# Grouping output stores on a saturated DMA queue: two stores of eight heads at every sixteenth head, in place of one at every eighth

## The chip, the cores and the metric

One core of a Trainium2 chip. The time is the device time of one execution in microseconds (us); the median of several executions is quoted. A profile is one execution recorded by the hardware profiler; its span leaves out some 1.8 us of the execution's time. The core's engines go by their short names: PE multiplies and transposes, DVE, ACT and POOL are the vector, scalar and GpSimd engines, SP the sync engine. HBM is the chip's main memory.

## The reference

```
attn_weights: float32 [8, 12, 1024, 1024]     v: float32 [8, 12, 1024, 64]
out = einsum('bhqs,bhsd->bhqd', attn_weights, v)      # float32 [8, 12, 1024, 64]
```

There are 96 heads. Each is a 1024 x 1024 matrix times a 1024 x 64 matrix. The weights are 403 MB, V and the output 25 MB each, so nearly all of the traffic is weights.

## The kernel before

The kernel takes four heads at a time (`q`, 24 steps) and loads their weights in two halves (`n`, 48 units), cast to bfloat16 on the way into two buffers `abf`. PE transposes each half, DVE and ACT copy the transposes out, PE multiplies and transposes back, and ACT copies the results into `osb`, a ring of ten slots of four heads each. POOL issues all transfers in the loop on one queue: weights, V for eight heads, and the output stores of eight heads (two slots).

```python
    HELD_FROM = NV - 8          # 16; NV = 24 steps of four heads
    BY_SYNC = NV - 4
    RING = 5                    # five pairs of slots
    ...
        def store(q, fours, eng, done):
            eng.wait_ge(s_out, 2 * (q + fours) + 1)
            at_slot = osb[:, ds(slot(q), fours)].rearrange("p n r d -> p n (r d)")
            eng.dma_start(
                out=out_2[q // 2] if fours == 2 else out_q[q],
                in_=at_slot if fours == 2 else at_slot[:, 0],
                **({"single_packet": True} if eng is pool else {}),
            ).then_inc(done, 16)

        def store_2(q):
            store(q, 2, pool, s_osb[q // 2 % 2] if q < HELD_FROM else s_held)
    ...
        for n in range(NU - 2):                       # POOL
            q, i = n // 2, n % 2
            if i == 0 and q % 2 == 1 and q + 1 < NV:
                for s in s_sp:
                    pool.wait_ge(s, 2 * q + 2)
                load_v((q + 1) // 2)
            pool.wait_ge(s_t[True], (n + 1) * PER_DVE)   # unit n is transposed, its buffer is free
            load_attn(n + 2)
            if i == 0 and q % 2 == 0 and 0 < q <= HELD_FROM:
                store_2(q - 2)
        for q in range(HELD_FROM, BY_SYNC, 2):
            store_2(q)
    ...
        nc.sync.sem_inc(s_free, RING)                 # SP
        for n in range(-2, NU - 2):
            ...
            nc.sync.sem_inc(s_half)
            if n >= 0 and n % 2 == 0:
                q = n // 2
                ...
                if q % 2 == 1 and 1 < q <= HELD_FROM:
                    nc.sync.wait_ge(s_osb[(q - 3) // 2 % 2], 16 * ((q - 3) // 4 + 1))
                    nc.sync.sem_inc(s_free)
        store(NV - 4, 2, nc.sync, s_end)
        store(NV - 2, 1, nc.sync, s_end)
        ...                                           # three last stores of the last four heads
        for k in range(2):
            nc.sync.wait_ge(s_osb[k], 16 * (HELD_FROM // 4))
        nc.sync.wait_ge(s_held, 16 * (BY_SYNC - HELD_FROM) // 2)
        nc.sync.wait_ge(s_end, 16 * 5)
```

SP waits for completions and passes them on: `s_half` tells PE that a load is complete, `s_free` tells ACT that a pair of slots may be written again. Because SP waits on constants, its loop is unrolled.

Of the kernel before, what the change touches and what calls it, by code (L numbers as in the profile page):

```python
# [10 lines left out]
def kernel(  # L11
# [18 lines left out]
    nc = tc.nc  # L30
# [15 lines left out]
    VB = S // VP // SB  # L46
    NV = NH // VH
    NU = 2 * NV


    HELD_FROM = NV - 8
# [4 lines left out]

    HALVED = NU - 2

    def slot(q):
        return q % NO  # L60
# [20 lines left out]
    with tc.tile_critical(no_gpsimd_drain=True):  # L81
# [18 lines left out]
        s_abf = [sem(f"s_abf{i}") for i in range(2)]  # L100
        s_second = {n: sem(f"s_second{n}") for n in range(HALVED, NU)}
        s_v0, s_v = sem("s_v0"), sem("s_v")
        s_osb = [sem(f"s_osb{i}") for i in range(2)]
# [15 lines left out]
        s_half, s_free = sem("s_half"), sem("s_free")  # L119
# [33 lines left out]
        def transpose_back(parts=((0, 4, px[0]), (4, 4, px[1]))):  # L153
            for j0, jn, ps in parts:
                for j in range(jn):
                    last = pe.matmul(  # L156
                        out=ps[:, ds(j * P, P)],
                        lhsT=ot[:, j0 + j],
                        rhs=ident,
                        is_transpose=True,  # L160
                        start=(j == 0),
                        stop=(j == jn - 1),
                    )
                last.then_inc(s_back)
# [16 lines left out]
        def wait_both(s, n):  # L181
            for x in s:
                pe.wait_ge(x, n)

        def pe_unit(i, n, loaded, it):

            pe.wait_ge(*loaded)
            for g in range(G):
                if g == GH:
                    pe.wait_ge(s_half, n)  # L190
                transpose_g(abf[i], g, n)
            wait_both(s_ot, n)
            if i == 0:
                pe.wait_ge(s_vr, it)
                odd = pe.snap((it - 1) % 2)
                with pe.If(odd > 0):
                    spread_v(1, po + px)
                with pe.Else():
                    spread_v(0, po + px)
                wait_both(s_vbf, it * 2)  # L200
            transpose_back()
            wait_both(s_last, n)
            for hp in range(2):
                for h in range(2):
                    for half in range(2):
                        outs = po[hp][ds(half * D, D), ds(h * GH * VP, GH * VP)]
                        last = multiply(outs, 2 * hp + h, half)
                last.then_inc(s_m[hp])

        pe.wait_ge(s_const, 1 + VH)  # L210
        with nc.Fori(1, NV + 1, 1, engines=(PE,)) as it:
# [4 lines left out]
            pe_unit(1, second, (s_abf[1], loaded), it)  # L216
        wait_both(s_ot, NU + 1)
        transpose_back()


        def engine(dve):
# [11 lines left out]
            def back_copy(rows, j0, jn, ps, count):  # L233

                eng.wait_ge(s_back, count)
                return copy(  # L236
                    out=rows.rearrange("p (half j) d -> p j half d", half=2)[:, ds(j0, jn)],
                    in_=ps[:, ds(0, jn * P)].rearrange("p (j half d) -> p j half d", half=2, d=D),
                )
# [59 lines left out]
            rows = osb[:, slot(NV - 1), ds(G, G)]  # L299
            back_copy(rows, 4 * k, 4, px[k], 2 * NU + k + 1).then_inc(s_fin[k])  # L300

# [13 lines left out]
        def load_attn(n):  # L315
            pieces = [(0, G)] if n < HALVED else [(0, GH), (GH, GH)]
            for g0, gn in pieces:
                pool.dma_start(  # L318
                    out=abf[n % 2][:, ds(g0, gn)].rearrange("p g s -> p (g s)"),
                    in_=attn_q[n // 2][:, ds((n % 2 * G + g0) * S, gn * S)],  # L320
                ).then_inc(s_abf[n % 2] if g0 == 0 else s_second[n], 16)

        def load_v(iv):
            pool.dma_start(  # L324
                out=vr.rearrange("p two b x -> p two (b x)"), in_=v_2[iv]
            ).then_inc(s_v, 16)
# [12 lines that stand above are left out]
# [14 lines left out]
        for h in range(VH):  # L353
# [9 lines left out]
            ).then_inc(s_const)  # L363
        for n in range(NU - 2):
# [4 lines that stand above are left out]
                load_v((q + 1) // 2)  # L369
            pool.wait_ge(s_t[True], (n + 1) * PER_DVE)  # L370
            load_attn(n + 2)
            if i == 0 and q % 2 == 0 and 0 < q <= HELD_FROM:
                store_2(q - 2)
        for q in range(HELD_FROM, BY_SYNC, 2):
            store_2(q)
# [11 lines left out]
        nc.sync.sem_inc(s_free, RING)  # L387
        for n in range(-2, NU - 2):

            if n + 2 < HALVED:  # L390
                nc.sync.wait_ge(s_abf[n % 2], 16 * ((n + 2) // 2 + 1))
            else:
                nc.sync.wait_ge(s_second[n + 2], 16)
# [3 lines that stand above are left out]
                if q % 2 == 1 and q + 1 < NV:  # L397
                    nc.sync.wait_ge(s_v, 16 * ((q + 1) // 2))
                    nc.sync.sem_inc(s_vr, 2)
                if q % 2 == 1 and 1 < q <= HELD_FROM:  # L400
                    nc.sync.wait_ge(s_osb[(q - 3) // 2 % 2], 16 * ((q - 3) // 4 + 1))
                    nc.sync.sem_inc(s_free)
        store(NV - 4, 2, nc.sync, s_end)
        store(NV - 2, 1, nc.sync, s_end)
        rows = osb[:, slot(NV - 1)].rearrange("p (u half j) d -> p u half j d", u=2, half=2)
# [41 lines left out]
```

## Time and profile before

| | before |
|---|---|
| time, median of 3 | 1054.85 us (1054.56 to 1054.90) |
| span of the profiled execution | 1053.1 us |
| busiest compute engine | PE, 70% |
| share of the 16 DMA engines held by POOL's queue | 99.1% |
| HBM read / written | 427.82 / 25.17 MB |

The chain of waits is the view to read here. Each of its rows gives a start, a duration and what was waited for, so a row "DMA abf" ends (start plus duration) when a load of weights has landed. In mid-stream, every landing in the chain is that of the second half of a step of four heads, so between two lie two loads, with a V load, a store or nothing more. I call the distance between two landings an interval, and the time from the first landing in mid-stream (near 86.7 us) to the last load of weights the stream. Before, the first is 59.47 + 27.21 = 86.68, in a line that the prediction shows, and the last is

```profile
1001.80 29.87 DMA abf<-in_attn_weights_dram
```

at 1031.67, so the stream takes 944.97 us from the unrounded records. What follows it is the tail, in which the last 8.39 MB of output leave, and then the end, from the last completion to the last instruction.

### The profile page before, as it was taken

How to read it: one execution, taken by the hardware profiler on the slowest of the kernel's cores; microseconds unless marked ns; L12 is line 12 of the kernel's file. 1: busy time of each engine (PE TensorE's matmuls, PEld its weight loads, DVE VectorE, ACT ScalarE, POOL GpSimd, SP SyncE). 2: the span in 40 equal slices, each digit the busy share in tenths (PEclk: the TensorE clock that was granted, in tenths of full speed). 3: DMA queues.
4: the chain of work that ended last, by engine and by line, in shares of the span. 5: the costliest groups of instructions: out<-in, count | busy, mean ns of one | idle time of the engine just before them, and what ended most of it. 6: DMA issues, size and time to landing. Idle time of an engine off the chain costs nothing.

```text
span 1053.1 us, 16530 instructions
## 1 busy us (share of the span) xinstructions
PE 738.0 (70%) x6920; PEld 692.4 (66%) x6920; DVE 388.8 (37%) x582; ACT 410.3 (39%) x493; POOL 45.1 (4%) x80
## 2 busy tenths in 40 slices
PE   0787677676697568667768757765776866875885
PEld 0686676565686567656668657765766866865874
DVE  0453343333353234333334324433333433532542
ACT  0354344433353334333335334433333533533542
POOL 1000000000000000000000000000000000000000
PEclk9989888898798888889879888888887987988998
DMA  9999999999999999999999999999999999999998
GB/s 235 224 217 218 218 244 219 219 214 249 231 214 251 215 219 258 217 219 230 243 217 210 259 217 218 259 219 219 248 217 217 218 211 225 219 208 230 206 216 339
DMA packets 14330, 240.19 MB, mean 228 GB/s; under 512 B 1269, under 2 KB 1781, under 8 KB 4725
## 3 DMA queue, kind: packets, MB, share of 16 engines
q0 software_dynamic: 12912, 233.84, 99.1%
q1 hardware_dynamic: 1413, 6.29, 1.5%
q8 instruction: 2, 0.03, 0.0%
q14 instruction: 3, 0.02, 0.0%
HBM read 427.82 MB, written 25.17 MB: 430 GB/s over the span
## 4 chain that ended last, share of the span: by engine, by line
DMA 75%; PE 22%; issue 1%; DVE 0%; SPq 0%; ACT 0%; POOL 0%; DVEq 0%
DMA abf<-in_attn_weights_dram 72%; PE bank L129 21%; DMA osb<-in_v_dram 3%; PE bank L171 1%; PE bank L156 0%; DVE vbf L229 0%; SPq L384 0%; PE bank L144 0%; DVE at L250 0%; DVE osb L236 0%; ACT ot L262 0%; POOL abf L318 0%; DVEq L249 0%; DVE vr L308 0%; DVEq L283 0%
## 5 line engine op out<-in xcount | busy, mean ns | idle before, releaser
L129 PE MATMUL bank<-ident,abf 128*128 128x128 f32 x3072 | 454.1, 318 | 273.6 <-DMA abf<-in_attn_weights_dram 264.4
L129 PEld LDWEIGHTS bank<-ident,abf 128*128 128x128 f32 x3072 | 444.2, 214 | 286.8 <-DMA abf<-in_attn_weights_dram 276.2
L250 DVE COPY at<-bank 128x1024 bf16<-128x1024 bf16 x480 | 320.4, 689 | 463.8 <-PE bank L129 460.0
L250 ACT COPY at<-bank 128x1024 bf16<-128x1024 bf16 x288 | 288.8, 1012 | 419.9 <-PE bank L129 419.9
L171 PE MATMUL bank<-at,vbf 128*64 128x256 bf16 x3072 | 215.0, 278 | 0.0
L171 PEld LDWEIGHTS bank<-at,vbf 128*64 128x64 bf16 x3072 | 196.8, 108 | 13.4 <-DVE at L250 4.0
L262 ACT COPY ot<-bank 128x512 f32<-128x512 f32 x48 | 28.1, 586 | 174.2 <-PE bank L171 174.2
L262 DVE COPY ot<-bank 128x512 f32<-128x512 f32 x48 | 33.2, 692 | 151.3 <-PE bank L171 151.3
L156 PE MATMUL bank<-ident,ot 128*128 128x128 f32 x392 | 52.2, 276 | 32.9 <-DVE vbf L229 32.1
L156 PEld LDWEIGHTS bank<-ident,ot 128*128 128x128 f32 x392 | 43.4, 141 | 45.0 <-DVE vbf L229 43.9
L236 ACT COPY osb<-bank 128x512 f32 (+1 forms) x97 | 52.2, 589 | 27.1 <-PE bank L156 26.3
L318 POOL DMA_DIRECT2D abf<-in_attn_weights_dram x50 | 27.3, 546 | 692.4 <-PE bank L129 691.4
L229 DVE CAST vbf<-bank 128x512 bf16<-128x512 f32 x48 | 30.9, 686 | 6.5 <-PE bank L144 6.5
L229 ACT CAST vbf<-bank 128x512 bf16<-128x512 f32 x48 | 25.8, 589 | 11.8 <-PE bank L144 11.8
L144 PE MATMUL bank<-vr,spread 32*128 32x512 bf16 x384 | 25.8, 377 | 0.0
L324 POOL DMA_DIRECT2D vr<-in_v_dram x11 | 7.8, 706 | 234.9 <-PE bank L144 234.9
L250 ACT ACT_TABLE_LOAD x12 | 15.4, 1283 | 1.3 <-SPq L81 1.1
L144 PEld LDWEIGHTS bank<-vr,spread 32*128 32x128 bf16 x384 | 10.2, 92 | 6.7
L308 DVE CAST vr<-osb 128x4096 bf16<-128x4096 f32 x1 | 2.3, 2294 | 30.4 <-DMA osb<-in_v_dram 30.4
L331 POOL DMA_DIRECT2D out_dram<-osb x10 | 7.2, 717 | 30.4 <-ACT osb L236 30.4
L355 POOL TENSOR_SCALAR_AFFINE_SELECT spread<-spread 32x512 bf16<-32x512 bf16 x4 | 2.5, 631 | 0.6
L236 DVE COPY osb<-bank 128x512 f32<-128x512 f32 x1 | 0.7, 692 | 3.1 <-PE bank L156 3.1
(8 smaller groups left out, 2.1 us busy)
## 6 DMA issues: line engine op xcount, KB each, us to landing
abf<-in_attn_weights_dram POOLq DMA_DIRECT2D x46, 4096.0 KB, 33.3
out_dram<-osb POOLq DMA_DIRECT2D x10, 2048.0 KB, 29.5
vr<-in_v_dram POOLq DMA_DIRECT2D x11, 1024.0 KB, 17.2
abf<-in_attn_weights_dram POOLq DMA_DIRECT2D x4, 2048.0 KB, 24.4
out_dram<-osb SPq DMA_DIRECT2D x1, 2048.0 KB, 13.7
osb<-in_v_dram SPq DMA_DIRECT2D x1, 1024.0 KB
out_dram<-osb SPq DMA_DIRECT2D x1, 1024.0 KB, 15.8
osb<-in_v_dram SPq DMA_DIRECT2D x1, 768.0 KB
```

The lines of the kernel that those rows point to most:

```text
L129: last = pe.matmul(out=pt[g % 4][:, k], lhsT=words[:, k], rhs=ident, is_transpose=True, start=(k == 0), stop=(k == KW - 1),)
L144: last = pe.matmul(out=ps, lhsT=spread[rows, b], rhs=vr[rows, two, b], start=(b == 0), stop=(b == VB - 1),)
L156: last = pe.matmul(out=ps[:, ds(j * P, P)], lhsT=ot[:, j0 + j], rhs=ident, is_transpose=True, start=(j == 0), stop=(j == jn - 1),)
L171: last = pe.matmul(out=outs, lhsT=vbf[:, 2 * kw + par, h], rhs=at[:, ds(half * GH, GH), kw, ds(h * VP, VP), par], start=(n == 0), stop=(n ...
L229: copy(out=vbf[:, :, h], in_=ps.rearrange("p (k d) -> p k d", k=SB)).then_inc(s_vbf[e])
L236: return copy(out=rows.rearrange("p (half j) d -> p j half d", half=2)[:, ds(j0, jn)], in_=ps[:, ds(0, jn * P)].rearrange("p (j half d) -> ...
L250: ins = copy(out=at[:, g].rearrange("c k j two -> c (k j two)"), in_=bank[g % 4].bitcast(bf16),)
L262: copy(out=ot.rearrange("c j (h p) -> c h j p", h=VH)[:, ds(2 * e, 2)], in_=po[e].rearrange("c (h j p) -> c h j p", h=2, j=GH),).then_inc( ...
L318: pool.dma_start(out=abf[n % 2][:, ds(g0, gn)].rearrange("p g s -> p (g s)"), in_=attn_q[n // 2][:, ds((n % 2 * G + g0) * S, gn * S)],).th ...
L324: pool.dma_start(out=vr.rearrange("p two b x -> p two (b x)"), in_=v_2[iv]).then_inc(s_v, 16)
L331: eng.dma_start(out=out_2[q // 2] if fours == 2 else out_q[q], in_=at_slot if fours == 2 else at_slot[:, 0], **({"single_packet": True} if ...
L355: pool.affine_select(out=spread[ds(h * VP, VP)], in_=spread[ds(h * VP, VP)], compare_op=mybir.AluOpType.not_equal, fill=1.0, base=0, patte ...
```

## The change

The intent is to turn the DMA engines from loading to storing four times in the loop instead of eight. The bytes stay. SP's bookkeeping has to follow: it now waits for two stores and frees two pairs of slots at once.

```diff
-            if i == 0 and q % 2 == 0 and 0 < q <= HELD_FROM:
+            if i == 0 and q % 4 == 0 and 0 < q <= HELD_FROM:
+                store_2(q - 4)
                 store_2(q - 2)
...
-                if q % 2 == 1 and 1 < q <= HELD_FROM:
-                    nc.sync.wait_ge(s_osb[(q - 3) // 2 % 2], 16 * ((q - 3) // 4 + 1))
-                    nc.sync.sem_inc(s_free)
+                if q % 4 == 1 and 1 < q <= HELD_FROM + 1:
+                    for k in range(2):
+                        nc.sync.wait_ge(s_osb[k], 16 * (q // 4))
+                    nc.sync.sem_inc(s_free, 2)
```

## The prediction

> **What bounds the kernel now.** I first read the page's engine shares and DMA rows, then the chain of waits, then the timeline of POOL, which issues nearly every transfer.
>
> ```profile
> span 1053.1 us, 16530 instructions
> PE 738.0 (70%) x6920; PEld 692.4 (66%) x6920; DVE 388.8 (37%) x582; ACT 410.3 (39%) x493; POOL 45.1 (4%) x80
> ...
> q0 software_dynamic: 12912, 233.84, 99.1%
> ...
> HBM read 427.82 MB, written 25.17 MB: 430 GB/s over the span
> ```
>
> No compute engine is over 70%, while the queue that POOL feeds holds all 16 DMA engines for 99.1% of the span. 452.99 MB pass through HBM at 430 GB/s. The kernel is a stream of transfers, and work on the other engines is free unless it makes the stream pause.
>
> The chain of waits in order of time (start us, us, what) says how steady the stream is. Each "DMA abf" row ends when a load of weights has landed, so sums of start and duration are a clock: 59.47 + 27.21 = 86.68, 95.05 + 35.14 = 130.19, and so on.
>
> ```profile
> 59.47 27.21 DMA abf<-in_attn_weights_dram
> ...
> 95.05 35.14 DMA abf<-in_attn_weights_dram
> ...
> 139.97 34.49 DMA abf<-in_attn_weights_dram
> 174.47 0.04 issue
> 174.51 10.02 PE bank L129 x64
> 184.53 0.29 issue
> 184.81 33.19 DMA abf<-in_attn_weights_dram
> ...
> 226.37 35.61 DMA abf<-in_attn_weights_dram
> ...
> 795.50 33.03 DMA abf<-in_attn_weights_dram
> ...
> 836.89 30.29 DMA abf<-in_attn_weights_dram
> ```
>
> Between two such landings lie two loads of 8.39 MB (float32 in HBM) and either a V load of 2.10 MB, an output store of 2.10 MB, or, late in the kernel, nothing. The row of PE between them is not a cost: while PE transposes, the next load is already moving.
>
> The POOL timeline (start us, us, engine, line, operation, what) gives the queue's order:
>
> ```profile
> 95.05 0.53 POOL L318 DMA_DIRECT2D abf<-in_attn_weights_dram  x1 [14.19 <-PE bank L129]
> 120.61 0.53 POOL L318 DMA_DIRECT2D abf<-in_attn_weights_dram  x1 [25.02 <-PE bank L129]
> 124.94 0.71 POOL L331 DMA_DIRECT2D out_dram<-osb  x1 [3.80 <-ACT osb L236]
> 139.97 0.56 POOL L318 DMA_DIRECT2D abf<-in_attn_weights_dram  x1 [14.32 <-PE bank L129]
> 162.12 0.71 POOL L324 DMA_DIRECT2D vr<-in_v_dram  x1 [21.59 <-PE bank L144]
> ```
>
> The load issued at 139.97 lands at 174.46; the load issued at 120.61 and the store of 124.94 are ahead of it in the queue. So the interval 130.19 to 174.47 holds load, store, load; the next one, to 218.00, holds V, load, load.
>
> **What the Trainium skill says.** "DMA: Bandwidth & Descriptors", section "Where 436 GB/s comes from", puts the ceiling of a core's 16 DMA engines at 435 GB/s. The trace agrees: the interval without V or store, 828.53 to 867.18, is 38.65 us for 16.78 MB, 434 GB/s. So loads have nothing left to give. The same page, "Anatomy of one DMA", fits a fixed cost of about 2 us to each DMA, mostly waiting for the write's receipt. In this trace that is not visible on the stream, since other transfers are queued behind: a V interval costs only 4.9 us over the plain one (below), 0.07 us over its bytes. The section "Two DMAs through the same engine are not ordered" says that an engine's read and write sides are separate queues and pipelined, which fits such joins being nearly free. I found no page that gives a cost for turning from reading HBM to writing it; that cost is what the change could save, and only the trace can size it.
>
> **The change part by part.** *Bytes and instructions.* Ten POOL stores of 2048 KB before, ten after; no descriptor, load or compute instruction differs, as the instruction orders of the two kernels also show: only the places of the stores in POOL's order differ. Eight of the ten are in the loop (the two held ones are issued after the last load either way). After it, they come as four pairs: the queue reads load, store, store, load at every sixteenth head, where it read load, store, load at every eighth.
>
> *What a store costs the stream now.* The eight store intervals, from the chain, are 44.28, 43.97, 43.64, 43.59, 43.55, 43.72, 43.82 and 43.56 us: sum 350.13, mean 43.77. V intervals are 43.50 to 43.58, about 43.53. Plain ones are 38.64 and 38.62. So a V load costs 43.53 - 38.63 = 4.90 us and a store 43.77 - 38.63 = 5.14 us. At 434 GB/s, 2.10 MB need 4.83 us. A store thus has an excess of 0.31 us over its bytes and 0.24 over an equal load; eight stores 2.5 us over bytes, 1.9 us over loads. The completion records of single DMA engines in the trace show where it sits: the last of the 16 engines gets 0.1 to 0.4 us later in the load just ahead of most stores (the spread between first and last engine's completions grows from 1.14 us at 130.19 to 2.15 us at 785.01, stepwise at stores and never at V loads). That looks like a cost of the turn from reading to writing.
>
> *What halving the turns saves.* If the whole excess belongs to the turn and each pair pays it once, four of eight turns go: 4 x 0.24 to 4 x 0.31 = 0.95 to 1.25 us. If the excess belongs to the bytes written, nothing goes. The steps are uneven (0.75 us in the first store interval, 0.02 in the fifth), so they may depend on chance alignment. I take two thirds: about 0.8 us saved.
>
> *Waits.* POOL waited 8 times for ACT's copy before a store, 3.80 us each, 30.4 us in total in the waits. Of a pair, the first store's data are eight heads old and need no wait; the second has the old wait. Only four waits of 3.8 us stay: 15.2 us less POOL waiting, worth nothing on the path, since the next load's issue comes 15 us after the store anyway (139.97 against 124.94).
>
> *The handshake.* SP now frees two slots at once, after the pair, at every fourth step of four heads. ACT needs the first freed slot at the step of heads 40 to 43; it is freed two loads after the pair issued at the step of heads 16, about nine loads of over 19.3 us ahead. All later ones are similarly early (eight loads at least). ACT's waits on osb name only PE now (26.3 us, never a store) and should still.
>
> Sum: 1054.85 - 0.8 = about 1054.05 us.
>
> **The rivals.**
>
> *A. Turns are expensive and the pair hides one: a gain of several us.* Against: the whole excess of all eight stores is 2.5 us, so even removing all of it could not give 2%, which is 21 us. With half the turns, at most 1.25 us: 1053.6.
>
> *B. The longer block of writes starves the loads.* A pair is about 10 us in which no weights arrive. For: PE would idle that much longer before one unit. Against: PE already waits for loads 264 us in total; the weights' buffer can be refilled as soon as PE has transposed it (8 to 10.5 us), and the next load is then issued with half of the 19.3 us of the current one still to go, so the queue does not run dry. A pair makes that margin larger for the load behind it. In return, the intervals without a store have only loads: four loads at 19.3 us each; PE's work per unit is 738.0 / 48 = 15.4 us. The late stretch 785 to 867 runs like that now without a gap. Time: unchanged. A dry queue at each pair would have to add 5 us x 4 = 20 us even to reach 2%, and I see no mechanism.
>
> *C. Back-to-back writes are slower than single ones (a buffer toward HBM fills).* The end of the kernel has 8.39 MB of stores with nothing between: from the last weights at 1031.66 to the last completion at 1051.47 is 19.81 us, 423 GB/s, or 4.95 us per 2.10 MB, on par with 5.14 for a lone store. So at most +0.1 us per second store: 1055.2.
>
> *D. SP gets stuck on the pair's completion and releases the second half of a load late.* SP waits for the stores only after a load has landed that was queued two loads later, on the same queue; the stores are done by some 24 us by then. Time: unchanged.
>
> **Range and chances.** The mechanism bounds the saving at some 1.3 us (2.5 if all stray excess vanished), the losses at a few tenths, and three timed runs of before spread over 0.34 us. I expect 1054.05 us, with 1053.0 to 1055.2 holding it 8 times in 10. A move of 2% is 21 us, eight times the whole excess of all stores; for faster or slower by that much I leave 1% each, for something I have not seen, and 98% for within 2%.
>
> **What would show each step right or wrong.** In the chain of waits of after, intervals between landings should be about 43.5 (V), 38.6 (plain) and four of about 48.5 to 48.8 (pair: 38.63 + 2 x 4.83 + one turn of 0.3 = 48.6). A pair interval of 48.9 or more (38.63 + 2 x 5.14) would say that the excess goes with the bytes, and the saving is nil. The DMA share should stay at 99%, the totals of HBM traffic equal, POOL's wait for ACT fall to about 15 us, ACT's osb wait keep naming PE. The prediction is wrong if ACT waits for a store, if PE waits for SP in mid-kernel, if a DMA slice of the page falls below 9 in the middle, or if a plain interval becomes longer than 38.7 us.

## The result, and the profile after

| | before | after |
|---|---|---|
| time, median of 6 | 1054.80 us (1053.95 to 1055.22) | 1054.74 us (1054.38 to 1057.07) |
| span of the profiled execution | 1053.1 us | 1053.1 us |

The ratio of after to before is 1.0003, with a 95% interval of 0.999 to 1.0016. It is the ratio of the mean times, 1055.06 and 1054.71 us, so not quite that of the medians; one run of 1057.07 us pulls it above 1. The change made no difference that the clock shows.

The page of after, its totals first:

```profile
span 1053.1 us, 16527 instructions
...
q0 software_dynamic: 12912, 233.84, 99.0%
...
q14 instruction: 3, 0.02, 0.0%
HBM read 427.82 MB, written 25.17 MB: 430 GB/s over the span
```

Bytes and packets are those of before. There are three instructions fewer, which at first sight means nothing. (I come back to them and to the "instruction" queue.)

The chain of waits of after, with its columns start us, us, what:

```profile
57.50 28.99 DMA abf<-in_attn_weights_dram
...
176.97 35.25 DMA abf<-in_attn_weights_dram
...
220.58 40.20 DMA abf<-in_attn_weights_dram
...
271.27 33.05 DMA abf<-in_attn_weights_dram
...
312.68 30.29 DMA abf<-in_attn_weights_dram
...
352.80 33.72 DMA abf<-in_attn_weights_dram
...
394.88 40.29 DMA abf<-in_attn_weights_dram
...
1002.27 28.42 DMA abf<-in_attn_weights_dram
```

The landings are at 212.22, 260.78, 304.32, 342.97, 386.52 and 435.17. So a pair interval takes 48.56 us (260.78 - 212.22), a V interval 43.54, a plain one 38.65, and the next pair interval 48.65. The stream runs from 86.49 to 1030.69 and takes 944.20 us, 0.77 us less than before. That is the predicted saving, and the stream began 0.20 us earlier as well, yet the span is the same to 0.1 us. The time gained is spent after the stream.

POOL's timeline around the first pair and its wait in the list of waits (engine, line, waited for: us in total, times, longest):

```profile
203.21 0.53 POOL L319 DMA_DIRECT2D abf<-in_attn_weights_dram  x1 [25.72 <-PE bank L130]
203.73 0.71 POOL L332 DMA_DIRECT2D out_dram<-osb  x1
207.54 0.72 POOL L332 DMA_DIRECT2D out_dram<-osb  x1 [3.10 <-ACT osb L237]
220.58 0.55 POOL L319 DMA_DIRECT2D abf<-in_attn_weights_dram  x1 [12.32 <-PE bank L130]
```
```profile
POOL out_dram L332 <- ACT osb L237: 12.4, 4, 3.1
```
```profile
ACT osb L237 <- PE bank L157: 26.2, 25, 1.1
```

The first store of the pair goes out at once, the second waits 3.1 us for ACT, and the next load is issued 13 us later, with the queue full. ACT's only wait before writing `osb` is still for PE, never for a store.

Where the stream's gain went can be read from the records of completions and of SP's instructions in the trace (this is my own listing of them, not a profile view):

```
                               before     after
last weights landed           1031.66   1030.69
last store completed          1051.47   1051.00     tail 19.81 -> 20.31 us
last instruction              1053.11   1053.06     end   1.64 ->  2.06 us

SP instruction 79, counted from 0 in the profile:
before   issue of the last store      previous one ended 1045.04, this began 1045.46
after    branch after the last wait   previous one ended 1051.04, this began 1051.46
```

Half a microsecond went in the tail and 0.42 us at the end. The 0.42 us is a pause of SP ahead of its 80th instruction. The pause is there before, too, but before it delays the issue of a store that would have queued anyway (in b_hand, below, that store is issued 0.27 us earlier, and the tail is 19.80 us). In after SP has 90 instructions instead of 93, and the same pause falls behind the last completion, where everything waits for it.

### The profile page after: what moved, and what is told of

It reads as the page before. It is cut to its first block, busy times and chain, and to the rows that moved or that the text cites. A ratio compares the mean times of both kernels' runs of the same rounds, so it can differ in the third digit from the quotient of the medians. Undisturbed runs are those within 1.5% of the kernel's fastest.

```text
span 1053.1 us, 16527 instructions
## 1 busy us (share of the span) xinstructions
PE 725.6 (69%) x6920; PEld 679.8 (65%) x6920; DVE 387.9 (37%) x582; ACT 410.1 (39%) x493; POOL 45.0 (4%) x80
## 4 chain that ended last, share of the span: by engine, by line
DMA 76%; PE 22%; issue 1%; DVE 0%; SPq 0%; ACT 0%; POOL 0%; DVEq 0%
DMA abf<-in_attn_weights_dram 73%; PE bank L130 20%; DMA osb<-in_v_dram 3%; PE bank L172 1%; PE bank L157 0%; DVE vbf L230 0%; SPq L386 0%; PE bank L145 0%; DVE at L251 0%; DVE osb L237 0%; ACT ot L263 0%; POOL abf L319 0%; DVEq L250 0%; DVE vr L309 0%; DVEq L284 0%
## 5 line engine op out<-in xcount | busy, mean ns | idle before, releaser
L130 PE MATMUL bank<-ident,abf 128*128 128x128 f32 x3072 | 441.8, 313 | 284.8 <-DMA abf<-in_attn_weights_dram 279.5
L130 PEld LDWEIGHTS bank<-ident,abf 128*128 128x128 f32 x3072 | 431.9, 214 | 298.0 <-DMA abf<-in_attn_weights_dram 291.3
L332 POOL DMA_DIRECT2D out_dram<-osb x10 | 7.2, 719 | 12.4 <-ACT osb L237 12.4
```

Source lines behind the costliest of these rows:

```text
L130: last = pe.matmul(out=pt[g % 4][:, k], lhsT=words[:, k], rhs=ident, is_transpose=True, start=(k == 0), stop=(k == KW - 1),)
L332: eng.dma_start(out=out_2[q // 2] if fours == 2 else out_q[q], in_=at_slot if fours == 2 else at_slot[:, 0], **({"single_packet": True} if ...
```

## The experiments

The clock cannot resolve any of this: executions of one kernel differ by up to 2.7 us. The profiles can, since their intervals repeat within hundredths except where stores are. So each experiment is read from its profile, and its time is given beside it. The experiments ran in three groups on three chips, each beside a run of the kernel before; every group has profiles with lone stores and with pairs. Theories: the turn theory of the prediction (each turn from loading to storing has a price, which a pair pays once); the theory that the excess goes with the bytes stored or is chance; the place theory for the end (the pause belongs to a place in SP's instruction stream); and, later, that issuing a store early is what helps.

### a_again: the changed kernel once more

No edit.

> The changed kernel once more, to see whether the stream gain of its first profile repeats. Turn theory (each turn from loading to storing costs 0.24 to 0.31 us beyond the bytes, a pair pays it once): the four intervals with a pair again 48.5 to 48.75 us, time 0.7 to 1.0 us below before. No-effect theory (the excess goes with the bytes, or the steps of the first profile of before were chance): pair intervals 48.9 or more, or before's own intervals shorter this time; time within 0.3 us of before.

Measured: 1055.05 us (5 runs) against 1055.16 (9 runs), ratio 1.0. Pair intervals 48.44, 48.50, 48.63, 48.62; stream 943.79 us. The stream's gain repeats, and the time again does not show it.

### b_again: the kernel before against itself

No edit.

> The kernel before against itself: how far two sets of runs of one kernel lie apart, and whether its eight store intervals repeat. Turn theory: store intervals again average about 43.75 us, time within 0.2 us of before. Chance theory: the uneven steps (0.75 us in the first interval, 0.02 in the fifth) move or vanish, and the average store interval differs from 43.77 by more than 0.1.

Measured: 1054.61 us (1054.25 to 1056.39) against 1055.16, which is how far two sets of runs of one kernel lie apart. This was more than I expected. The mean store interval is 43.76 us, as in the first profile (43.77), and the stream 944.90. But the intervals with a large excess are others: the first has 0.02 us this time, the third 0.54. So the total repeats and its steps do not.

### apart: the same pairs, with a load between the two stores

```diff
-            if i == 0 and q % 4 == 0 and 0 < q <= HELD_FROM:
-                store_2(q - 4)
-                store_2(q - 2)
+            if q % 4 == 0 and 0 < q <= HELD_FROM:
+                store_2(q - 4 + 2 * i)
```

> The same two stores at every sixteenth head, but with one load of weights between them, so eight turns again while everything else of the change (late first store, two slots freed at once) stays. Turn theory: the gain goes, time equals before, 0.7 to 1.0 us above the changed kernel. If lateness or the handshake mattered: equal to the changed kernel. No-effect theory: all three equal within 0.3 us.

Measured: 1055.84 us against 1055.16, ratio 1.0004; stream 945.50 us, 1.3 to 1.7 above the two profiles of after, end 2.06 us. The chain of waits around the first two stores:

```profile
178.68 33.72 DMA abf<-in_attn_weights_dram
...
220.75 35.67 DMA abf<-in_attn_weights_dram
...
267.04 37.79 DMA abf<-in_attn_weights_dram
```

The landings are at 212.40, 256.42 and 304.83. Taking away only the adjacency takes away the stream's gain, so neither the lateness of the stores nor the handshake made it. The four intervals with the first store average 44.12 us, those with the second and V 48.40: the first store of each group costs 5.47 us over a plain interval and the second 4.86 over a V interval. A price per turn would have charged both the same.

### quad: four stores back to back

```diff
-            if i == 0 and q % 4 == 0 and 0 < q <= HELD_FROM:
-                store_2(q - 4)
-                store_2(q - 2)
+            if i == 0 and q % 8 == 0 and 0 < q <= HELD_FROM:
+                for k in (8, 6, 4, 2):
+                    store_2(q - k)
...
-                if q % 4 == 1 and 1 < q <= HELD_FROM + 1:
+                if q % 8 == 1 and 1 < q <= HELD_FROM + 1:
                     for k in range(2):
-                        nc.sync.wait_ge(s_osb[k], 16 * (q // 4))
-                    nc.sync.sem_inc(s_free, 2)
+                        nc.sync.wait_ge(s_osb[k], 32 * (q // 8))
+                    nc.sync.sem_inc(s_free, 4)
```

> Four stores back to back at every thirty-second head: two turns in place of eight. Turn theory: 6 x 0.24 to 0.31 = 1.4 to 1.9 us below before; the two intervals with four stores 38.63 + 4 x 4.83 + 0.3 = 58.3 us. Bytes theory: 38.63 + 4 x 5.14 = 59.2 us and time as before. If ACT ever waits for a slot (it has one unit to spare), a wait on a DMA shows on ACT and the time rises.

Measured: 1055.35 us against 1055.16, ratio 1.0002. The two intervals are 58.80 and 58.25 us, the stream 944.00. So four in a row gain over lone stores (0.9 us) but nothing over pairs in the stream, and the expected 1.4 to 1.9 did not come. The end is 2.14 us. SP has 88 instructions here, and number 79 is a DRAIN two instructions further on, with a pause of 0.44 us ahead of it. That made the place theory likely.

### a_pad: the changed kernel with three idle SP instructions

```diff
+        s_pad = sem("s_pad")
...
+                if q in (3, 7, 11):
+                    nc.sync.sem_inc(s_pad)
                 if q % 4 == 1 and 1 < q <= HELD_FROM + 1:
```

> The changed kernel with three idle semaphore increments added to SP, so that SP again executes 93 instructions instead of 90. In the traces so far SP's instruction number 79 (counted from 0) always starts 0.4 us late: in before it is the issue of the last store, hidden behind queued stores; in the changed kernel the branch after the last completion. Place theory: the pause moves back to the last store, the distance from the last store's completion to the end of the span falls from 2.06 to about 1.64 us, and the time is 0.4 us below the changed kernel, 0.8 to 1.2 below before where the stream gain holds. Rival (the late branch comes from the new handshake or from when completions come): the distance stays at 2.06.

Measured: 1054.57 us against 1054.71, ratio 1.0. The end is 1.64 us, with SP's instruction 79 being the issue of the last store again. The place theory holds in this direction. The stream is 943.63 us, the shortest with correct stores, but the tail is 20.65 us, so the last completion still comes at 1051.12 and the expected gain of 0.8 to 1.2 us against before is not there. To the last instruction, this profile takes 965.92 us from the landing near 86.7, the least of the correct kernels (quad takes 965.95); its difference in time from before lies inside the noise, and it was not timed beside the changed kernel.

### b_hand: the new handshake alone

```diff
-                if q % 2 == 1 and 1 < q <= HELD_FROM:
-                    nc.sync.wait_ge(s_osb[(q - 3) // 2 % 2], 16 * ((q - 3) // 4 + 1))
-                    nc.sync.sem_inc(s_free)
+                if q % 4 == 1 and 1 < q <= HELD_FROM + 1:
+                    for k in range(2):
+                        nc.sync.wait_ge(s_osb[k], 16 * (q // 4))
+                    nc.sync.sem_inc(s_free, 2)
```

> The kernel before with SP's new handshake alone (two slots freed at once), stores in the old places: 90 SP instructions. Place theory: end distance 2.06 us as in the changed kernel, stream between first and last weights 944.9 us as before, time 0.4 us above before. Rival (the pairs on the queue cause the late end): end distance 1.64 us, time as before.

Measured: 1055.11 us (1055.03 to 1055.73) against 1054.71; the interval of the ratio, 0.9991 to 1.0018, still spans 1. End 2.06 us and stream 944.93, both as expected; tail 19.80. So half of the change, by itself, costs 0.42 us at the end of the profile. With a_pad, which undoes it by three idle instructions, this leaves the number of SP's instructions as the cause.

### single: sixteen stores of four heads

```diff
-            if i == 0 and q % 2 == 0 and 0 < q <= HELD_FROM:
-                store_2(q - 2)
+            if i == 0 and 0 < q <= HELD_FROM:
+                store(q - 1, 1, pool, s_osb[(q - 1) // 2 % 2])
...
-                    nc.sync.wait_ge(s_osb[(q - 3) // 2 % 2], 16 * ((q - 3) // 4 + 1))
+                    nc.sync.wait_ge(s_osb[(q - 3) // 2 % 2], 32 * ((q - 3) // 4 + 1))
...
-            nc.sync.wait_ge(s_osb[k], 16 * (HELD_FROM // 4))
+            nc.sync.wait_ge(s_osb[k], 32 * (HELD_FROM // 4))
```

> The kernel before with a store of four heads at every fourth head: sixteen bursts of 1 MB in place of eight of 2 MB. Turn theory: eight turns more at 0.24 to 0.31 us, so stream 946.9 to 947.4 us against 944.9 and time 2.0 to 2.5 us above before. Bytes theory: stream within 0.6 us of before (eight more transfers at 0.07 us, as V loads show).

Measured: 1054.90 us against 1054.71, ratio 1.0003. The stream is 944.75 us, where the turn theory wanted 946.9 to 947.4. The first four intervals in the chain of waits, all with a store of 1 MB, every other one with V as well:

```profile
56.24 30.62 DMA abf<-in_attn_weights_dram
...
96.67 36.72 DMA abf<-in_attn_weights_dram
...
143.80 31.50 DMA abf<-in_attn_weights_dram
...
185.12 36.17 DMA abf<-in_attn_weights_dram
...
232.07 30.32 DMA abf<-in_attn_weights_dram
```

The landings are at 86.86, 133.39, 175.30, 221.29 and 262.39, the intervals 46.53, 41.91, 46.00 and 41.10. The later ones are all like the last two. A store of 1 MB there costs 41.10 - 38.65 = 2.45 us, and its bytes at the rate of the loads need 2.42. Fourteen turns at this price cost almost nothing, and the first two cost some 1.4 us together. A fixed price per turn is ruled out.

### reads: loads in place of stores (wrong on purpose)

```diff
-                store_2(q - 2)
+                pool.wait_ge(s_out, 2 * q + 1)
+                pool.dma_start(
+                    out=osb[:, ds(slot(q - 2), 2)].rearrange("p n r d -> p n (r d)"),
+                    in_=v_2[q // 2 - 1],
+                ).then_inc(s_osb[(q - 2) // 2 % 2], 16)
```

> Wrong on purpose: each of the eight stores in the loop is a load of 2 MB of V into the same slot, under the same waits, so the direction never turns and the outputs of those heads are not written. Turn theory: all those intervals 43.53 us as V's, stream 944.9 - 8 x 0.24 = 943.0, and the spread between DMA engines stays as it was at the first weights. Rival (the excess comes from the place in the queue, or from the wait for ACT): intervals stay at 43.75.

Measured: 1053.86 us (1053.45 to 1054.37) against 1054.71, ratio 0.9992; the result is wrong, as intended. The chain of waits:

```profile
96.64 33.74 DMA abf<-in_attn_weights_dram
...
138.74 35.19 DMA abf<-in_attn_weights_dram
...
183.58 33.89 DMA abf<-in_attn_weights_dram
```

From 130.38 to 173.93 there is the transfer in a store's place, 43.55 us, and from there to 217.47 a V load, 43.54. All eight are 43.55. The stream is 943.35 us (943.0 was expected), and the spread between the DMA engines at its end, 1.46 us, is what it was at its beginning, 1.51; before, it grew from 1.18 to 2.16. So the excess does come from the direction, storing in place of loading; the place in the queue and the wait for ACT, which are the same here, add none. All that the direction costs with eight lone stores is 944.97 - 943.35 = 1.6 us, the most that any grouping of the same bytes could save in the stream.

### single_again, old and a_late: one look each

single_again is single without an edit. old issues each lone store one step later, right behind the load and without a wait for ACT; a_late puts both stores of a pair behind that wait:

```diff
-            if i == 0 and q % 2 == 0 and 0 < q <= HELD_FROM:        # old, against before
-                store_2(q - 2)
+            if i == 0 and q % 2 == 0 and 4 <= q <= HELD_FROM + 2:
+                store_2(q - 4)
...
-                if q % 2 == 1 and 1 < q <= HELD_FROM:
-                    nc.sync.wait_ge(s_osb[(q - 3) // 2 % 2], 16 * ((q - 3) // 4 + 1))
+                if q % 2 == 1 and 4 < q <= HELD_FROM + 2:
+                    nc.sync.wait_ge(s_osb[(q - 5) // 2 % 2], 16 * ((q - 5) // 4 + 1))
```
```diff
             if i == 0 and q % 4 == 0 and 0 < q <= HELD_FROM:        # a_late, against after
+                pool.wait_ge(s_out, 2 * q + 1)
                 store_2(q - 4)
```

> The sixteen bursts once more, for its profile, since its first one contradicted a fixed price per turn (stream 944.75 us, 1.34 us of excess in the first two store intervals and almost none in the other fourteen). If the price per turn is really not fixed: stream between 944 and 945.2 us again, most intervals 45.99 and 41.10. If that profile was lucky: 946.9 to 947.4.

Measured: 1055.17 us, one run each, against 1055.39. Stream 945.09 us, most intervals again 45.99 to 46.0 and 41.1, the excess now in the first, second, fourth, fifth and sixth. The price per turn is not fixed.

> The kernel before with each lone store one step later (data eight heads older), so that it is issued with no wait for ACT, right behind the load. Still eight lone stores, at the 24th to the 80th head. If what the pairs gain comes from the earlier issue: store intervals fall to 43.53 to 43.6 and the stream to about 943.6 us. If it comes from having fewer places where stores meet loads: mean store interval stays at 43.7 to 43.8, stream about 944.9.

Measured: 1055.11 us against 1055.39; mean store interval 43.78 us, stream 945.26. Issuing lone stores early does not help.

> The changed kernel with both stores of a pair behind the wait for ACT, so none is issued early. If early issue matters: pair intervals of 48.7 to 49.0 and stream 944.7 to 945. If fewer places matter: pair intervals 48.5 to 48.65 as before, stream 943.6 to 944.2. SP has 90 instructions, so the end distance should be 2.06 us in any case.

Measured: 1054.48 us against 1055.39; stream 943.97 us, end 2.06. The four pair intervals are 48.44, 48.48, 47.96 and 48.82; the third is short because the two intervals ahead of it ran 0.2 and 0.5 us long, the one disturbance of this kind in these profiles. Pairs that are issued late keep the gain. So it is not the earlier issue.

### All together

All from the profiles, in us. "To last store" is from the landing near 86.7 to the last completion.

| kernel | places x stores | stream | to last store | tail | SP instructions | end |
|---|---|---|---|---|---|---|
| before | 8 x 1 | 944.97 | 964.79 | 19.81 | 93 | 1.64 |
| b_again | 8 x 1 | 944.90 | 964.72 | 19.82 | 93 | 1.64 |
| b_hand | 8 x 1 | 944.93 | 964.73 | 19.80 | 90 | 2.06 |
| old | 8 x 1 | 945.26 | 965.06 | 19.80 | 93 | 1.64 |
| single | 16 x 1/2 | 944.75 | 964.56 | 19.81 | 93 | 1.64 |
| single_again | 16 x 1/2 | 945.09 | 964.90 | 19.81 | 93 | 1.64 |
| apart | 8 x 1 | 945.50 | 965.31 | 19.81 | 90 | 2.06 |
| after | 4 x 2 | 944.20 | 964.52 | 20.31 | 90 | 2.06 |
| a_again | 4 x 2 | 943.79 | 964.11 | 20.32 | 90 | 2.06 |
| a_pad | 4 x 2 | 943.63 | 964.28 | 20.65 | 93 | 1.64 |
| a_late | 4 x 2 | 943.97 | 963.98 | 20.01 | 90 | 2.06 |
| quad | 2 x 4 | 944.00 | 963.81 | 19.81 | 88 | 2.14 |
| reads | none | 943.35 | 963.57 | 20.22 | 93 | 1.64 |

The four profiles with lone stores at every eighth head (before, b_again, b_hand, old) have a mean stream of 945.02 us, the four with pairs 943.90: pairs gain 1.1 us there, and within each group of runs the pairs' stream is the shorter one too (943.79 against 944.90, 943.63 against 944.93, 943.97 against 945.26). Up to the last store the means are 964.82 and 964.22, so 0.6 us is left. At the end the changed kernel loses 0.42. What remains is about 0.2 us in 1054, and the clock cannot see it.

## Why the prediction was right, and where it was not

It was right about the outcome: no change within 2%, and 1054.74 us lies in its range, 0.7 us above the time that it expected. That range also holds "no change at all", so the time confirms nothing of the saving: the clock shows 0.06 us of the expected 0.8. Step by step:

- **What bounds the kernel.** Right. The DMA queue holds the engines at 99.0% after as well, and the plain and V intervals are 38.65 and 43.54 us in every kernel, to some hundredths (the last plain one, 38.75, was as long before, and two in a_late are longer). The 434 GB/s that the prediction sets beside the skill's 435 count the bytes read from HBM. The profile's own rate counts the bytes after the cast to half the size: 213 GB/s for loads alone in after (828 to 866 us). In reads, a load of 2.10 MB that is not cast costs the same 4.90 us as one of V that is. So the rate goes with the bytes read, and that the ports into SBUF, from which the skill works out its figure, are the limit here is not shown by the agreement of the numbers.
- **The cost of a store now.** Right in size. Three further profiles with lone stores at every eighth head give mean store intervals of 43.74 to 43.78 us, and reads shows that eight stores cost 1.6 us more than eight equal loads (1.9 was worked out).
- **What halving the turns saves.** The number held and its reason fell. Pair intervals of 48.6 us were foreseen; 48.56 to 48.70 were measured in the first profile, and the stream's gain is 0.77 there and 1.1 in the means, against 0.8. The two thirds that gave 0.8 were a guess, so the closeness of 0.77 is luck. And a turn has no fixed price: sixteen stores of half the size cost the stream no more than eight (single, single_again), four in a row no less than pairs (quad). What the runs support is narrower: the excess arises when stores meet loads, unevenly, in other places from run to run; it shows in part as some of the 16 engines falling behind (the spread grew by 0.98 us over the stream of before, but by 0.30 in b_again, with nearly the same excess); and putting two stores together at fewer places leaves less of it. Why is open.
- **Waits.** Right in kind: 12.4 us of POOL's waiting remain, where 15.2 were worked out from 3.8 us each (it is 3.1 now), and they cost nothing.
- **The handshake.** Right that ACT would never wait for a slot. Wrong that only the places of POOL's stores differ and that the rest costs nothing: the handshake takes three instructions from SP, which moves SP's pause behind the last completion. That is 0.42 us, shown by b_hand and undone by a_pad.
- **The sum.** It left out two terms, the 0.42 us of the end and what the tail gives back. The tail took 19.80 to 19.82 us in all seven profiles with lone stores, and 20.01 to 20.65 in the four with pairs. It ends with the slowest engine, and with pairs the engines enter it less spread (1.3 to 1.9 us against 1.8 to 3.2). Pairs as such are not the cause: quad enters with 2.2 us and took 19.81, and reads, with no store in the loop, enters with 1.5 and took 20.22. Nor is the spread alone: 1.81 in b_again went with 19.82, 1.84 in after with 20.31. No run separates the cause of the longer tail, so this term, 0.5 us, is measured and not explained.
- **The rivals.** A (a gain of several us) could not come, since reads bounds all of it at 1.6 us. B (starved loads) did not happen: V and plain intervals behind the pairs are unchanged. C (slower writes back to back) did not: a pair costs 48.65 - 38.65 = 10.0 us, two lone stores 10.28. D (SP stuck) did not show: PE waited for SP twice in either profile, 5.4 us in total before and 3.9 after, both times for the last loads (after 1010 us). The margin was even larger than the prediction's 24 us: the first pair had landed at 241.6 us, and SP freed its slots at 285.1.

## What to carry to other kernels

On a queue that is never empty, find out first what all of the suspected cost amounts to: here replacing stores with equal loads bounds it at 1.6 us, 0.15% of the time, before any regrouping is tried. A saving in mid-stream has to be followed to the last completion and to the last instruction, since tail and end can give it back. And where the expected effect is smaller than the spread of the clock, intervals in the profile of several executions can still decide it; one profile alone would have made the turn theory look confirmed.

## What the Trainium skill lacked or had wrong

- "Runtime: NRT & Kernel Launch", section "Instruction fetch mechanics", says that the sequencer refills its instruction memory by itself, in blocks of 16 KiB, and that the cost of crossing a boundary is "one DMA tail-bump, mostly hidden". The runs fit a cost of that kind and size it: 0.42 us (0.44 in quad) ahead of SP's instruction 79 in all 13 traces, whichever instruction that is. A packet of 8192 bytes on the instruction queue q14 follows it (at 1052.10 us in after, 0.6 us after the pause; at 1048.67 in before, 3.2 us after), which is not 16 KiB; packets of 16384 bytes are there too, two on queue q8, at 51.38 and 61.08 us in before. Behind the last completion the pause is not hidden. That the pause is this crossing is an inference from these times.
- "DMA: Bandwidth & Descriptors" has nothing on stores among loads. Here eight lone stores of 2.10 MB cost the stream 1.6 to 1.9 us more than loads of the same size (2.2 in apart), sixteen of half the size 1.4 to 1.7 us, four pairs 0.3 to 0.9 us, two groups of four 0.7 us, all against the one profile of reads.
- The same page, section "Anatomy of one DMA", fits some 2 us of fixed cost to each DMA. On a queue that stays full it does not appear: the last fourteen stores of 1.05 MB in single cost 2.44 to 2.46 us each, some 0.03 us over their bytes at the rate of the loads.
